# A hybrid attention layer: PSUM banks, activation tables and the place of four kinds of work on the engines

## The chip, the cores and the metric

One core of a Trainium2 chip runs the kernel; the other seven do nothing. The metric is the device time of one launch in microseconds, the median of three runs. Engines, as the profile names them: PE (TensorE, matrix products, with PEld for its weight loads), DVE (VectorE), ACT (ScalarE), POOL (GpSimd) and SP (SyncE, which here issues every DMA).

## The reference

x has 4096 rows of 1024 columns. It is modulated, `h = x * (1 + scale) + shift`, with shift, scale and a gate from `c @ w_ada + b_ada`, and projected by `h @ w_in` (3608 columns). Two kinds of attention run over chunks, each with 4 heads on half the width:

- Gated attention: `g = log_sigmoid(z) / 16` decays a state per key column. With b the running sum of g in a chunk of 64, the output is `tril((q e^(b-bref)) (k e^(bref-b))^T) v + (q e^b) S`, and `S = e^(b_last) S + (k e^(b_last-b))^T v`.
- Delta rule: q, k, v pass a causal convolution of width 4 and Silu, q and k are normalised; one decay per head and step. With `L = exp(d_i - d_j)` under the diagonal, `A = (beta k k^T) * L` strictly under it, each chunk solves `(A + I) [u, w] = [v beta, k beta e^d]`, then `v_new = u - w S`, `o = (q e^d) S + (q k^T * L) v_new`, `S = e^(d_last) S + (k e^(d_last-d))^T v_new`.

Each head's output is divided by its root mean square and multiplied by a weight and `silu` of a gate projection. Both halves together go through `w_out`, and the result is `layer_norm(alpha x + (1 + gate) y)`. All in float32.

## The kernel before, in words

The sequence is cut into 8 blocks of 512 rows (`NB`, `TB`). Products of the projections are made in three passes over a high and a low part of each operand (`mm3`), eight slices of 128 columns per sum (`KT`); one step of a query, key or convolution projection is three matrix products of 512 columns. PSUM has 8 banks; `share_banks` (L57) splits them into projection banks and work banks.

Phase 1, gated attention: 16 blocks, first all 8 with t = 0 (heads 0 and 1), then all 8 with t = 1. For t = 0, `make_h` (L213) loads x in four tiles, `mod_split` (L201) modulates each slice and splits it into two parts, and `keep_h` writes h to DRAM for the 24 later reads (`load_h`, L225). `block` (L586) makes values, then the gate's low-rank rows `lr` (transposed for t = 0 and stored; loaded and cast for t = 1), `decays` (the exponentials), queries, keys and gates, and ends in two Silus of `sg`. `chunks` (L488) and `finish` (L511) do the recurrence of the block before: eight chunk steps, each a product whose result one copy on DVE writes into the next step's operand and one copy on ACT into o; then sums of squares on ACT, a power on POOL, four transposes per half and the product with the gate. `first_block` (L537) makes block 0's eight sums while the modulation's weights and x arrive; its eight banks are three projection and five work banks.

Phase 2, the delta rule: again 16 blocks, each over several iterations. In iteration `it`, block `it` is new, block `it-1` is solved and scanned, block `it-2` is normalised. `first_half` (L989) is woven with the key and query projections (`qk_products`, 32 steps), `second_half` (L1010) with values and gates (`vg_products`). The tile E holds L of the new block: a load, a mask on POOL, eight exponentials on ACT (`decay_tiles`, L743); `gram` (L790) multiplies it into the products AQ, whose diagonal blocks are inverted on DVE after a round trip through DRAM (U, R, Rd). `inverse_head` and `inverse` (L835, L848) put the inverse together from small products, with copies of Pa and Rt on ACT between them; `scan` (L898) runs the recurrence.

Phase 3: products with `w_out`, and the layer norm per 128 rows (`out_block`, L682).

What sets the order: `weave` (L243) takes a generator of side work and one of projections; a side yield of n lets n projection steps pass before the side's next products. On PE the side's products are kept behind the projection products written before them while the projections last. ACT's functions of different tables are kept in written order (`in_order`, L82); a table that the written code does not load is loaded just ahead of its use. All else, every queue's order included, is chosen when the kernel is built by a scheduler that takes the written order, free buffers and its own durations; on the chip each engine then runs its queue in that order, and SP issues DMAs in its order. A tile whose tag has one buffer waits until the last reader of the tile before it is done: `lr_raw` shares the tag `la` with e1 (L394, L417), E and U share `EU`.

Of the kernel before, what the change touches and what calls it, by code (L numbers as in the profile page):

```python
# [13 lines left out]
F32 = mybir.dt.float32  # L14
# [16 lines left out]
def tile_hybrid(ctx, tc, xp, x, c, wada, bada, w_gla, w_vl, w_gdn, w_out, wup, bgate,  # L31
# [78 lines left out]

    def copy_a(out, in_):
        nc.scalar.copy(out=out, in_=in_)  # L112
# [88 lines left out]
    def mod_split(xt, k):  # L201
        j = k % 2
        nc.vector.tensor_scalar(out=xt[:, j], in0=xt[:, j], scalar1=modc[:, 8 + k:9 + k],
                                scalar2=modc[:, k:k + 1], op0=mul, op1=add)
        t = pair(hpool)
        return split(xt[:, j], (t[:, 0], t[:, 1])), t
# [6 lines left out]
    def make_h(b):  # L213
        h, tiles = [], []
        for kk in range(4):
            xt = xpool.tile([P, 2, TB], F32, name="xt", tag="x")
            nc.sync.dma_start(out=xt, in_=xp[b, kk])
            for j in range(2):
                parts, t = mod_split(xt, 2 * kk + j)
                h.append(parts)  # L220
                tiles.append(t)
        keep_h(b, tiles)
        return h
# [111 lines left out]
    with ExitStack() as ph:  # L335
        share_banks(ph, 3)
# [48 lines left out]
        def lr_rows(t, b):  # L385
            lr = gp.tile([80, TB], F32R, name="lr", tag="lr")
            if t == 0:
                pt = work_psum()
                for g in range(4):
                    transpose(pt[0:80, g * P:(g + 1) * P], in_=lrt[:, g].bitcast(F32), identity=ident)  # L390
                copy_a(lr, pt[0:80])
                nc.sync.dma_start(out=lrsp[b], in_=lr.bitcast(F32))
            else:
                raw = gp.tile([P, TB], F32, name="lr_raw", tag="la")[0:80]  # L394
                nc.sync.dma_start(out=raw, in_=lrsp[b])
                copy_a(lr, raw)
            return lr
# [74 lines left out]
        def values(t, b, wv, h, VS):  # L472

            nw = 256 if t else 280
            for gg in range(2):
                vps = [proj_psum() for _ in range(2)]
                for k in range(KT):
                    for j in range(2):
                        values_k(vps[j][:, 0:nw], wv, h, k, 2 * gg + j)
                    yield  # L480
                for j in range(2):
                    v_out(t, b, VS, 2 * gg + j, vps[j])
# [5 lines left out]
        def chunks(W, VS, VS_next, o, ss):  # L488

            o8 = o.rearrange("p g (h v) -> p (g h) v", h=2)  # L490
            for n in range(8):
                g, r = n // 2, n % 2
                pm = work_psum()
                for hh in range(2):
                    mm(pm[:, hh * P:(hh + 1) * P], lhsT=W[:, g, r, hh, :],
                                     rhs=VS[:, g, r, hh * P:(hh + 1) * P], start=True, stop=True)
                if r == 0:
                    nc.vector.tensor_copy(out=VS[0:64, g, 1, :], in_=pm[0:64, 0:256])  # L498
                    copy_a(o[64:128, g, :], pm[64:128, 0:256])
                else:  # L500
                    if g < 3:
                        nc.vector.tensor_copy(out=VS[64:128, g + 1, 0, :], in_=pm[64:128, 0:256])  # L502
                    elif VS_next is not None:
                        nc.vector.tensor_copy(out=VS_next[64:128, 0, 0, :], in_=pm[64:128, 0:256])
                    copy_a(o[0:64, g, :], pm[0:64, 0:256])
                    for j in (2 * g, 2 * g + 1):
                        jk = gp.tile([P, P], F32, name="jk", tag="jk")
                        act(jk, o8[:, j], AF.Square, accum_out=ss[:, j:j + 1])
                yield 2
# [25 lines left out]
        small = []  # L535

        def first_block():  # L537

            h, tiles, wt = [], [], {}
            ps = [proj_psum() for _ in range(3)] + [work_psum() for _ in range(8 - 3)]  # L540
            xt = None
            for k in range(KT):
# [18 lines left out]
                tiles.append(t)  # L561
            keep_h(0, tiles)
# [23 lines left out]
        def block(t, b, h, W, VS, sg, first):  # L586
# [11 lines left out]
            e1, e2, e3, e4 = decays(t, lr_rows(t, b))  # L598
# [10 lines left out]
            kt_, kh = scale_k(pk, e2, e4)  # L609
            pg = [proj_psum() for _ in range(2)] if first is None else first[6:8]  # L610
# [12 lines left out]
        def before(st, VS):  # L623
# [4 lines left out]
            yield from chunks(st["W"], st["VS"], VS, o, ss)  # L628
# [7 lines left out]
        for it in range(2 * NB + 1):  # L636
# [10 lines left out]
            if new:  # L647
# [5 lines left out]
                h = make_h(it + 1) if it + 1 < NB else load_h((it + 1) % NB)  # L653
# [28 lines left out]
    def out_block(b, y, xres, lnw_sb, lnb_sb):  # L682
        for g in range(4):
# [23 lines left out]
            nc.vector.tensor_scalar(out=xt, in0=xt, scalar1=mv[:, 0:1], scalar2=rl, op0=sub, op1=mul)  # L707
            tt(xt, xt, lnw_sb, mul)
            tt(xt, xt, lnb_sb, add)
            nc.sync.dma_start(out=out[r0:r0 + P], in_=xt)  # L710


    with ExitStack() as ph:
# [29 lines left out]
        def decay_tiles(t, b, E):  # L743
# [3 lines left out]
            load_table()  # L747
            for cc in range(2):
# [4 lines left out]
                for n in range(4 * cc, 4 * cc + 4):  # L753
                    act(E[:, n], E[:, n], AF.Exp, bias=dneg[:, t, c0 + n:c0 + n + 1])
# [93 lines left out]
        def inverse(st):  # L848
# [15 lines left out]
            yield 2  # L864
# [124 lines left out]
        def first_half(new, last, done):  # L989
# [15 lines left out]
            if last is not None:  # L1005

                yield 4 if done is not None else 10
                yield from inverse(last)

# [145 lines left out]
```

## Time and profile before

| what | value |
|---|---|
| median of three runs | 2152.29 us (2149.45 to 2164.0) |
| the profiled execution | 2148.5 us, span of the trace 2146.8 us |
| PE busy | 2064.2 us, 96% of the span |
| DVE busy | 1320.7 us, 62% |
| ACT busy | 956.6 us, 45% |
| POOL busy | 228.1 us, 11% |
| mean granted clock of PE | 0.988 of full speed |

The span runs from the first to the last instruction. A busy time is the union of an engine's instructions; matrix products overlap in the pipeline, so idle time of PE in this table is time in which it had nothing to run. In the page's 40 slices, gated attention fills about the first 13 (to some 700 us), the delta rule the next 22 (to some 1860 us), and the output the rest.

### The profile page before, as it was taken

The numbers are of one execution on the slowest core, as the hardware profiler recorded it, in microseconds if no ns is written. First come the engines' busy times: TensorE is split into PE (matmuls) and PEld (weight loads), VectorE is DVE, ScalarE is ACT, GpSimd is POOL, SyncE is SP. The second block draws the span as 40 slices with busy tenths as digits, with TensorE's granted clock in tenths as the row PEclk, the third lists the DMA queues.
The fourth block names the chain that finished last, engine by engine and source line by source line (L and its number), as shares of the span: only waits on it lengthen the run. The fifth ranks groups of instructions, "written<-read, shape, count | busy, mean of one in ns | idle before, by whom it ended". The sixth has DMA issues, their size and how long they took to land.

```text
span 2146.8 us, 34571 instructions
## 1 busy us (share of the span) xinstructions
PE 2064.2 (96%) x12809; PEld 1743.0 (81%) x12809; DVE 1320.7 (62%) x3181; ACT 956.6 (45%) x2563; POOL 228.1 (11%) x430
## 2 busy tenths in 40 slices
PE   6899999999999999999999999999999999999998
PEld 5788888888888778887888878888888888788886
DVE  7785666445335676655666666665566666676665
ACT  2655555544454544554535665445544463121110
POOL 1000000000000221111210212101221110000000
PEclk9999999999999999998999999999999999999999
DMA  8575336423423544331332443333123354353321
GB/s 316 193 254 203 141 134 227 157 102 107 168 92 118 203 172 163 95 96 46 114 116 92 139 151 104 116 103 95 56 94 116 124 182 140 140 210 143 136 103 76
DMA packets 118585, 297.17 MB, mean 138 GB/s; under 512 B 45920, under 2 KB 48144, under 8 KB 117392
## 3 DMA queue, kind: packets, MB, share of 16 engines
q1 hardware_dynamic: 118416, 294.95, 40.1%
q8 instruction: 101, 1.65, 0.3%
q14 instruction: 68, 0.56, 0.1%
HBM read 213.84 MB, written 81.07 MB: 137 GB/s over the span
## 4 chain that ended last, share of the span: by engine, by line
PE 64%; DVE 11%; ACT 9%; DMA 8%; issue 3%; POOL 2%; SPq 2%; POOLq 0%; DVEq 0%; ACTq 0%
PE pp L98 48%; PE pw L98 15%; DMA lr_raw<-lr_spill 2%; ACT jk L104 2%; PE pw L101 2%; DMA xt<-xp 2%; ACT E L104 2%; DMA r_spill<-R 1%; DVE tp L69 1%; DVE R L69 1%; ACT L104 1%; DVE vp L69 1%; DMA Rd<-r_spill 1%; DVE cacc L72 1%; DVE W L69 1%
## 5 line engine op out<-in xcount | busy, mean ns | idle before, releaser
L98 PE MATMUL pp<-h,w 128*128 128x512 f32 x4512 | 1158.9, 402 | 1.2 <-DVE W L69 1.2
L98 PEld LDWEIGHTS pp<-h,w 128*128 128x128 f32 x4512 | 824.1, 189 | 157.8 <-issue 2.0
L98 PE MATMUL pp<-w,h 128*128 128x512 f32 (+1 forms) x2112 | 421.5, 355 | 11.8 <-ACT sg L104 10.6
L98 PEld LDWEIGHTS pp<-w,h 128*128 128x128 f32 x2112 | 349.1, 189 | 65.7 <-ACT sg L104 12.0
L72 DVE SCALAR_TENSOR_TENSOR cacc<-u,convw_sb,cacc 128x512 f32<-128x512 f32 x288 | 217.4, 756 | 127.0 <-ACT cacc L104 122.2
L98 PE MATMUL pp<-wvl,h 128*128 128x280 f32 x744 | 119.9, 310 | 34.9 <-ACT h L112 26.3
L98 PEld LDWEIGHTS pp<-wvl,h 128*128 128x128 f32 x744 | 105.6, 198 | 38.7 <-ACT h L112 29.4
L69 DVE TENSOR_TENSOR tp<-U,R 128x60 f32<-128x60 f32 (+24 forms) x496 | 104.3, 210 | 14.7 <-DMA U<-u_spill 3.0
L69 DVE TENSOR_TENSOR R<-R,tp 128x60 f32<-128x60 f32 (+24 forms) x496 | 104.2, 210 | 12.8
L498 DVE COPY VS<-pw 64x256 f32<-64x256 f32 x64 | 26.7, 417 | 135.5 <-PE pw L98 135.1
L112 ACT COPY u<-pp 128x512 f32<-128x512 f32 x96 | 55.9, 582 | 119.8 <-PE pp L98 109.9
L104 ACT ACTIVATE rl<-mv,lnepscol 128x1 f32<-128x1 f32 x32 | 9.4, 294 | 217.9 <-DVE mv L703 215.8
L261 POOL TENSOR_TENSOR rs<-ss,minus_half 128x8 f32<-128x8 f32 x16 | 31.4, 1962 | 606.7 <-DVE ss L514 606.7
L98 PE MATMUL pw<-S,KQ 128*128 128x128 f32 x512 | 84.4, 278 | 0.0
L98 PE MATMUL pw<-VS,W 128*128 128x128 f32 x512 | 81.3, 282 | 1.2 <-DVE VS L498 0.9
L104 ACT ACTIVATE jk<-pw 128x128 f32<-128x128 f32 x256 | 70.5, 276 | 26.5 <-PE pw L101 20.3
L72 DVE SCALAR_TENSOR_TENSOR S<-S,edl,pw 128x128 f32<-128x128 f32 x128 | 42.4, 344 | 61.6 <-PE pw L98 61.5
L98 PEld LDWEIGHTS pw<-S,KQ 128*128 128x128 f32 x512 | 74.0, 191 | 6.3 <-DVE S L72 2.4
L104 ACT ACTIVATE jk<-vp 128x128 f32<-128x128 f32 x128 | 39.9, 311 | 84.7 <-DVE vp L69 82.7
L72 DVE SCALAR_TENSOR_TENSOR xres<-xres,pp 128x512 f32<-128x512 f32 x48 | 32.4, 684 | 70.9 <-PE pp L98 66.7
L112 ACT COPY o<-pw 64x256 f32<-64x256 f32 x128 | 46.8, 366 | 63.7 <-DVE VS L502 33.8
L98 PEld LDWEIGHTS pw<-VS,W 128*128 128x128 f32 x512 | 70.6, 196 | 4.2 <-DVE VS L502 0.9
(287 smaller groups left out, 2759.0 us busy)
## 6 DMA issues: line engine op xcount, KB each, us to landing
h<-h_spill SPq DMA_DIRECT2D x192, 512.0 KB
h_spill<-h SPq DMA_DIRECT2D x64, 512.0 KB
xt<-xp SPq DMA_DIRECT2D x32, 512.0 KB
y_spill<-sg SPq DMA_DIRECT2D x32, 512.0 KB
yt<-y_spill SPq DMA_DIRECT2D x32, 512.0 KB
xres<-x SPq DMA_DIRECT2D x24, 512.0 KB
out_dram<-xres SPq DMA_DIRECT2D x24, 512.0 KB
mt<-wada SPq DMA_DIRECT2D x8, 1024.0 KB
```

The costliest lines, as they stand in the source:

```text
L69: nc.vector.tensor_tensor(out=out, in0=a, in1=b, op=op)
L72: nc.vector.scalar_tensor_tensor(out=out, in0=a, scalar=s, in1=b, op0=op0, op1=op1)
L98: pe(nc.tensor.matmul(out, lhsT=lhsT, rhs=rhs, start=start, stop=stop))
L101: pe(nc.tensor.transpose(out, in_=in_, identity=identity))
L104: ins = nc.scalar.activation(out=out, in_=in_, func=func, **kw)
L112: nc.scalar.copy(out=out, in_=in_)
L261: nc.gpsimd.tensor_tensor(out=y, in0=x, in1=e, op=ALU.pow)
L498: nc.vector.tensor_copy(out=VS[0:64, g, 1, :], in_=pm[0:64, 0:256])
```

## The change

Gated attention: four projection banks and four work banks instead of three and five, and the first block's value sums take the four work banks; the Silu table is loaded right behind the exponentials; the modulation of x moves from DVE to ACT; `lr` is loaded without a cast for t = 1, and its store for t = 0 comes behind `scale_k`; values are made as one pair of groups and two single ones; squares move from ACT to POOL with a sum on DVE; a chunk step lets 3 projection steps pass for t = 0 (before 2). Two x loads of block 1 are issued ahead of the stores of block 0's h. Delta rule: the eight exponentials of E and their table load move from the place of the mask to the end of the first half; one yield of the inverse is 3 instead of 2. Output: the normalisation is two operations instead of three, and in halves for the last 128 rows.

```diff
@@ -107,6 +107,9 @@
         in_order(nc.scalar.preload_act_table_set("natural_log_exp_and_others"))
+    def load_silu():
+        in_order(nc.scalar.preload_act_table_set("silu_and_others"))
@@ -200,8 +203,7 @@
         j = k % 2
-        nc.vector.tensor_scalar(out=xt[:, j], in0=xt[:, j], scalar1=modc[:, 8 + k:9 + k],
-                                scalar2=modc[:, k:k + 1], op0=mul, op1=add)
+        act(xt[:, j], xt[:, j], AF.Identity, scale=modc[:, 8 + k:9 + k], bias=modc[:, k:k + 1])
@@ -210,11 +212,15 @@
-    def make_h(b):
+    def load_x(b, kk):
+        xt = xpool.tile([P, 2, TB], F32, name="xt", tag="x")
+        nc.sync.dma_start(out=xt, in_=xp[b, kk])
+        return xt
+    def make_h(b, ahead=()):
         for kk in range(4):
-            xt = xpool.tile([P, 2, TB], F32, name="xt", tag="x")
-            nc.sync.dma_start(out=xt, in_=xp[b, kk])
+            xt = ahead[kk] if kk < len(ahead) else load_x(b, kk)
@@ -333,7 +339,7 @@
     with ExitStack() as ph:
-        share_banks(ph, 3)
+        share_banks(ph, 4)
@@ -389,11 +395,8 @@
                 copy_a(lr, pt[0:80])
-                nc.sync.dma_start(out=lrsp[b], in_=lr.bitcast(F32))
             else:
-                raw = gp.tile([P, TB], F32, name="lr_raw", tag="la")[0:80]
-                nc.sync.dma_start(out=raw, in_=lrsp[b])
-                copy_a(lr, raw)
+                nc.sync.dma_start(out=lr.bitcast(F32), in_=lrsp[b])
@@ -472,22 +475,27 @@
             nw = 256 if t else 280
-            for gg in range(2):
-                vps = [proj_psum() for _ in range(2)]
+            vps = [proj_psum() for _ in range(2)]
+            for k in range(KT):
+                for j in range(2):
+                    values_k(vps[j][:, 0:nw], wv, h, k, j)
+                yield
+            for j in range(2):
+                v_out(t, b, VS, j, vps[j])
+            for g in range(2, 4):
+                ps = proj_psum()
                 for k in range(KT):
-                    for j in range(2):
-                        values_k(vps[j][:, 0:nw], wv, h, k, 2 * gg + j)
-                    yield
-                for j in range(2):
-                    v_out(t, b, VS, 2 * gg + j, vps[j])
+                    values_k(ps[:, 0:nw], wv, h, k, g)
+                    if k % 2:
+                        yield
+                v_out(t, b, VS, g, ps)
-        def chunks(W, VS, VS_next, o, ss):
-            o8 = o.rearrange("p g (h v) -> p (g h) v", h=2)
+        def chunks(W, VS, VS_next, o, ss, steps):
@@ -503,10 +511,11 @@
                     copy_a(o[0:64, g, :], pm[0:64, 0:256])
-                    for j in (2 * g, 2 * g + 1):
-                        jk = gp.tile([P, P], F32, name="jk", tag="jk")
-                        act(jk, o8[:, j], AF.Square, accum_out=ss[:, j:j + 1])
-                yield 2
+                    sq = gp2.tile([P, 2, P], F32, name="sq", tag="sq")
+                    o2 = o[:, g].rearrange("p (h v) -> p h v", h=2)
+                    nc.gpsimd.tensor_tensor(out=sq, in0=o2, in1=o2, op=mul)
+                    nc.vector.tensor_reduce(out=ss[:, 2 * g:2 * g + 2], in_=sq, op=add, axis=mybir.AxisListType.X)
+                yield steps
@@ -532,12 +541,12 @@
-        small = []
+        small, x_next = [], []
             h, tiles, wt = [], [], {}
-            ps = [proj_psum() for _ in range(3)] + [work_psum() for _ in range(8 - 3)]
+            ps = [work_psum() for _ in range(4)] + [proj_psum() for _ in range(4)]
@@ -559,6 +568,7 @@
                 tiles.append(t)
+            x_next.extend(load_x(1, kk) for kk in range(2))
@@ -595,7 +605,9 @@
                     v_out(t, b, VS, g, first[g])
-            e1, e2, e3, e4 = decays(t, lr_rows(t, b))
+            lr = lr_rows(t, b)
+            e1, e2, e3, e4 = decays(t, lr)
+            load_silu()
@@ -607,6 +619,8 @@
             kt_, kh = scale_k(pk, e2, e4)
+            if t == 0:
+                nc.sync.dma_start(out=lrsp[b], in_=lr.bitcast(F32))
@@ -625,7 +639,7 @@
             yield 2
-            yield from chunks(st["W"], st["VS"], VS, o, ss)
+            yield from chunks(st["W"], st["VS"], VS, o, ss, 2 if st["t"] else 3)
@@ -650,7 +664,7 @@
                     gate_scalars()
-                h = make_h(it + 1) if it + 1 < NB else load_h((it + 1) % NB)
+                h = make_h(it + 1, x_next if it == 0 else ()) if it + 1 < NB else load_h((it + 1) % NB)
@@ -704,10 +718,11 @@
             act(rl, rl, AF.Exp, scale=-0.5)
-            nc.vector.tensor_scalar(out=xt, in0=xt, scalar1=mv[:, 0:1], scalar2=rl, op0=sub, op1=mul)
-            tt(xt, xt, lnw_sb, mul)
-            tt(xt, xt, lnb_sb, add)
-            nc.sync.dma_start(out=out[r0:r0 + P], in_=xt)
+            for cs in [slice(0, D)] if r0 + P < T else [slice(0, TB), slice(TB, D)]:
+                stt(xt[:, cs], xt[:, cs], mv[:, 0:1], lnw_sb[:, cs], sub, mul)
+                stt(xt[:, cs], xt[:, cs], rl, lnb_sb[:, cs], mul, add)
+                nc.sync.dma_start(out=out[r0:r0 + P, cs], in_=xt[:, cs])
@@ -744,14 +759,17 @@
             nc.sync.dma_start(out=E.rearrange("p n c -> p (n c)"), in_=dsp[t, b:b + 1].to_broadcast([P, 8 * P]))
-            load_table()
                                         pattern=[[0, 4], [1, P]], channel_multiplier=-1)
-                for n in range(4 * cc, 4 * cc + 4):
-                    act(E[:, n], E[:, n], AF.Exp, bias=dneg[:, t, c0 + n:c0 + n + 1])
+        def decay_exps(t, b, E):
+            c0 = 8 * b
+            load_table()
+            for n in range(8):
+                act(E[:, n], E[:, n], AF.Exp, bias=dneg[:, t, c0 + n:c0 + n + 1])
@@ -861,7 +879,7 @@
                 copy_a(Pa[q[2 * i + 1]], pp[i][q[2 * i + 1]])
-            yield 2
+            yield 3
@@ -1006,6 +1024,8 @@
                 yield from inverse(last)
+            if new is not None:
+                decay_exps(new["t"], new["b"], new["E"])
```

## Rows read from the trace of the kernel before

**Rows 1.** Stretches: length; busy PE, PEld, DVE, ACT, POOL (count); clock; DMA share, GB/s.

```profile
61.50:84.00 22.50, 15.35 (x111) 14.05 (x112) 20.16 (x39) 14.55 (x25) 0.00 (x0) 0.77 0.65 227
...
150.00:370.00 220.00, 213.00 (x1430) 186.35 (x1429) 146.21 (x324) 124.49 (x279) 8.99 (x8) 0.99 0.47 174
370.00:700.00 330.00, 317.48 (x2117) 280.28 (x2116) 142.20 (x280) 154.64 (x383) 18.05 (x8) 0.99 0.36 128
...
872.00:1860.00 988.00, 974.38 (x6344) 811.74 (x6342) 628.74 (x1813) 483.95 (x1425) 151.57 (x321) 0.99 0.36 114
...
sum 2146.80, PE 2064.21 PEld 1743.01 DVE 1320.68 ACT 956.62 POOL 228.09; mean PE 229.36 PEld 193.67 DVE 146.74 ACT 106.29 POOL 25.34
```

**Rows 2.** PE's waits: us in total, times, longest us.

```profile
PE pw L98 <- ACT Pa L112: 11.5, 15, 1.6
PE pp L98 <- ACT sg L104: 10.6, 7, 2.5
PE pp L98 <- ACT o L112: 6.4, 4, 2.1
```

**Rows 3.** Timeline, a block's end, t = 1: start, duration, instruction, count [idle before <-releaser].

```profile
501.60 0.62 ACT L112 CAST lr<-lr_raw 80x512 fp32r<-80x512 f32 x1 [5.59 <-DMA lr_raw<-lr_spill]
502.24 1.28 ACT L104 ACT_TABLE_LOAD   x1
503.54 1.09 ACT L104 ACTIVATE sg<-pp 128x512 f32<-128x512 f32 x2
...
504.18 0.98 PE L98 MATMUL pp<-w,h 128*128 128x256 f32 x6 [1.12 <-ACT sg L104]
```

**Rows 4.** Timeline, 202 to 217 us, ACT in the values, t = 0.

```profile
212.67 0.62 ACT L112 CAST h<-xt 128x512 fp32r<-128x512 f32 x1 [0.99 <-DMA xt<-xp]
```

**Rows 5.** Groups by form: shapes, busy us, mean ns, idle before.

```profile
L104 ACT ACTIVATE la<-la,onecol 128x512 f32<-128x512 f32 x16 | 11.5, 720 | 0.3
```

**Rows 6.** Timeline, 0 to 70 us, DVE beside POOL.

```profile
11.47 1.67 DVE L203 TENSOR_SCALAR xt<-xt,modc 128x512 f32<-128x512 f32 x1
11.49 1.36 POOL L360 TENSOR_TENSOR wvl<-raw,wvl 128x560 fp32r<-128x560 f32 x1 [8.48 <-ACT wvl L112]
```

**Rows 7.** Timeline, 2128 to 2147 us and 2143 to 2147 us, the end.

```profile
2137.58 0.69 DVE L72 SCALAR_TENSOR_TENSOR xres<-xres,pp 128x512 f32<-128x512 f32 x1 [3.96 <-PE pp L98]
...
2139.84 0.81 DVE L707 TENSOR_SCALAR xres<-xres,mv,rl 128x1024 f32<-128x1024 f32 x1 [0.60 <-ACT rl L104]
...
2143.19 0.33 SPq L710 DMA_DIRECT2D out_dram<-xres  x1
```

**Rows 8.** Timeline, 505 to 512 us, chunk steps (t = 1).

```profile
506.87 0.43 DVE L502 COPY VS<-pw 64x256 f32<-64x256 f32 x1 [0.80 <-PE pw L98]
...
508.10 0.61 PE L98 MATMUL pw<-VS,W 128*128 128x128 f32 x4
```

**Rows 9.** Timeline, 54 to 90 us, from_q of block 0.

```profile
69.57 1.73 DVE L69 TENSOR_TENSOR W<-pw,e 64x256 f32<-64x256 f32 x4
```

**Rows 10.** Timeline, 1108 to 1142 us, ACT ahead of Pa.

```profile
1126.68 1.28 ACT L109 ACT_TABLE_LOAD   x1
...
1127.97 2.46 ACT L104 ACTIVATE E<-E,dneg 128x128 f32<-128x128 f32 x8
...
1134.15 1.28 ACT L104 ACT_TABLE_LOAD   x1
...
1136.77 0.60 PE L98 MATMUL pw<-Rd,Pa 32*32 32x32 f32 x9 [1.17 <-ACT Pa L112]
```

**Rows 11.** Timeline, 1142 to 1175 us, last KQ and first AQ.

```profile
1142.78 0.62 ACT L104 ACTIVATE KQ<-cacc 128x512 f32<-128x512 f32 x1
...
1144.25 1.66 DVE L72 SCALAR_TENSOR_TENSOR AQ<-pw,f__11191,E 128x256 f32<-128x256 f32 x4 [3.50 <-PE pw L98]
```

**Rows 12.** Busy time of ACT, granted clock, 1143.4 to 1154.4 us.

```profile
1143.40:1154.40 11.00, 4.53 (x20) 1.00 0.21 48
```

**Rows 13.** Busy time of each engine and granted clock, 998 to 1014 us.

```profile
998.00:1014.00 16.00, 14.86 (x103) 11.61 (x104) 5.89 (x13) 5.41 (x13) 1.96 (x3) 0.57 0.00 1
```

## The prediction

> **What bounds the kernel now.** I read the stages first: TensorE is busy 2064.21 us of a 2146.80 us span [rows 1], so all its waiting together is 82.6 us, and no edit on another engine can give more than its share of that. By stage: 7.2 us of waiting in 61.5 to 84 (end of the first block), 7.0 in 150 to 370 (gated attention, t = 0), 12.5 in 370 to 700 (t = 1), 13.6 in 872 to 1860 (delta rule). The rest is the start, which waits for the first loads, the end behind the last product, and places that the change does not aim at. Then TensorE's waits by who ended them [rows 2]: leaving aside the h tiles, most of which are the first ones, three ScalarE tiles lead, Pa (11.5 us in 15 waits), sg (10.6 us in 7) and o (6.4 us in 4). The change touches what stands ahead of each on ScalarE's queue.
>
> **The change part by part.**
>
> *Gated attention, t = 1 (sg).* At a block's end ScalarE casts the loaded rows lr (waiting 5.59 us for their load), loads the Silu table (1.28) and runs the two Silus (1.09); TensorE has one free bank, fills it with 12 products and then stands 1.12 us until the first Silu frees one [rows 3]. The change takes away all three causes: the load goes straight into lr (the cast is gone, and the load has its own tile, no longer the one that e1 holds until the block's end), the Silu table is loaded behind the exponentials, and a fourth bank lets the next values start. I take the whole sg wait, 10.6 us. What is late next: nothing on ScalarE before the next o copy. The fourth bank is taken from the work banks (5 to 4); the largest need at once is three in from_k, or two at the gate transposes.
>
> *t = 0 (o).* A cast of the next h, held 0.99 us by its x load, stands ahead of the VS and o copies on ScalarE, and those free banks [rows 4]. With four projection banks no values group waits for an earlier group's copy, and at three steps a chunk instead of two the state copy has one more step of six products; 6.4 us of o waits would go, I take 6. Moving the modulation puts 64 operations more on ScalarE. Nearest rows: the cast of 80x512 at 0.62 [rows 3] and a 128x512 operation with one column operand at 0.72 [rows 5]; a second column operand may add the same 0.10 again, so 0.62 to 0.82, I take 0.72, the nearer in kind: 5.8 us a block. The squares that leave are not counted against it. ScalarE is busy 124.49 of 220 us there [rows 1], so this is hidden; if that cover were gone it would cost 8 blocks x 5.8 = 46. The loads of x now stop ScalarE instead of VectorE, and behind them stand the copies just named; the fourth bank is what covers that.
>
> *Squares on GpSimd.* By elements, 256/560 of the 1.36 us row gives 0.62 us for each of 64, then a VectorE sum near 0.4. GpSimd is nearly idle. The price is on VectorE: its modulation of 128x512 took 1.67 us beside the GpSimd operation that began 0.02 later [rows 6], where another operation of that size takes 0.69 [rows 7], so a VectorE operation can be held for all of it. Where it hit a state copy of a chunk: the copy of 0.43 us starts at 506.87 and the chunk that reads it at 508.10 [rows 8], a slack of 0.80, more than 0.62. I take 0, bound 3 us.
>
> *First block.* Two x loads of block 1 are issued ahead of eight h_spill issues, but its value banks are now work banks and the query, key and gate sums hold all four projection banks. Block 1 can start only when from_q has read the queries (its last read ended at 71.30 [rows 9]) or a Silu has read a gate; VectorE no longer modulates, so about 70. Before, block 1 had banks early and stood for h. So the two edits work against each other: of 7.2 us I take 2, between -3 and +7. The lr_spill store moves behind scale_k on SyncE's queue; its reader comes eight blocks later, so 0. The spill of the gated output issues later for t = 0, since chunks and finish take 8 more steps; x loads queued behind it wait for tiles freed at the same time, 0, bound 4 us over 7 blocks.
>
> *Delta rule, exponentials last.* In the first half ScalarE runs, without a gap, table load 1.28, eight exponentials 2.46, then copies and squares, table load 1.28, Silu, and only then the Pa copies; TensorE stands 1.17 us for them at 1136.77 [rows 10]. That is 5.02 us ahead of Pa that leave. The waits for Pa are 1.6 at most each, so all 11.5 us go; I take 11. Where they come back: the chain is now fourth KQ Silu's end 1143.40, load to 1144.68, first pair of exponentials 1145.30, last 1147.14. The products AQ that read E start at 1144.25 after VectorE had been idle 3.50 us [rows 11]; they would be 1.05 late, and no more at the end, since a product takes 0.42 and an exponential 0.31. ScalarE is idle 11.00 - 4.53 = 6.5 us between that Silu and the z copy at 1154.40 [rows 12], more than 5.02. So 0, with a bound of 5.02 in each of 15 blocks. The step of the inverse raised from 2 to 3 does nothing: by then the side has taken 31 steps (10+1+1, 1+1, 3, 8, 2, 4) of 32, and both 2 and 3 run the main part out.
>
> *Clock.* In 998 to 1014 the granted clock is 0.57 [rows 13], part of it at the lower level of 1.2 GHz, after a Pa wait of 1.6 us; at 0.57 a stretch of 16 us loses up to 6.9. Other waits of that size show no fall, so I count 3 of it, between 0 and 7.
>
> *Tail.* From 2139.84 to the issue at 2143.19 three operations; now two of 0.69 for each half [rows 7]: 4 x 0.69 = 2.8 against 3.35, with the first no longer waiting for rl and the last store half as large, so 1 us. The other row blocks' shorter normalisation is hidden by products.
>
> *Sum:* 10.6 + 6 + 2 + 11 + 3 + 1 = 33.6, 34 us, on a profiled execution of 2148.5 us (span 2146.8): 2114.5. The median shown is 2152.29, 3.8 above that execution, so I predict 2118.
>
> **The rivals.** *The waits move (no change).* The order on each engine is chosen anew at build time, so other operations may meet; the fall of o and sg may give way to ScalarE standing for x with Silu and copies behind it. The cast of [rows 4] speaks for it, the idle time of ScalarE and the fourth bank against. If the t = 0 gain and the first block's are lost (8), VectorE's collisions cost 3 and a fifth of the 46 us shows (9), 34 - 8 - 3 - 9 = 14 us are left: about 2138. *The exponentials become the bound (slower).* Place: AQ waits for E, the gram sums keep four of five work banks, and the scan's products queue behind them. Price: 5.02 us in 15 blocks, 75 us, and the 11 + 3 us of gain gone: 2152.3 - 20 + 75 = 2207. It decides from 2.8 us a block ((21.5 + 20)/15); the idle 3.50 us ahead of AQ speaks against. *A table load holds ScalarE longer than its row (less gain).* Place: the two loads that now stand between the fourth Silu and the first vT. Over the 5.02 us there are 1.5 left; each us beyond comes back in 15 blocks, 15 us. In the row at 502.24 the Silu follows its load's end by 0.02 [rows 3], so this has a small chance, and at 1.3 us over the time would be 2118 + 20 = 2138. The Trainium skill (ScalarE: Activation LUTs, What ACT_TABLE_LOAD costs) gives each switch a drain of about 1.38 us besides its 1.28, so two of them would take 2.8 us more, 1.3 over what is left; the row does not show such a drain. *More than forecast:* all of the first block's 7, the whole 6.9 of clock, and the early loads too: 34 + 5 + 4 + some of the slow clock near 62 to 84 (granted 0.77, up to 5): about 2105 or below. *It does not do what it says:* for the inverse step and the early x loads that is my forecast already.
>
> **How the numbers follow.** About 1% (21.5 us) is what this measurement tells from no change: faster is below 2130.8, slower above 2173.8. Forecast (26 to 42 us gained, 2110 to 2126) 0.45; more than forecast 0.17; waits move, 2126 to 2152, 0.27, of which a sixth is still below 2130.8; longer loads 0.03; exponentials or another new bound 0.08. So faster 0.67, same 0.26, slower 0.07. Range: 2096 to 2146, which leaves out the slower case and the far ends of two others.
>
> **What would show it.** In t = 1, no sg wait on TensorE and no lr cast on ScalarE; in the delta rule, Pa copies right behind their products and no Pa wait, exponentials between the fourth Silu and the first vT, and AQ's first pair about 1 us later against its sums. TensorE idle in 872 to 1860 near 3 us, in 370 to 700 near 2. It would be wrong if TensorE waited for AQ, z or E in the second half, if ScalarE's modulation stood for x with VS or o copies behind it and TensorE behind those, or if block 1 started later than 73 us.

## The result and the profile after

The changed kernel took 2123.05 us (2120.95 to 2125.33, three runs) against 2152.29 before: ratio 0.9845, interval 0.9816 to 0.9875. The forecast was 2118 in 2096 to 2146. The profiled executions differ less, 2146.8 to 2123.6 us of span: the one shown after was the slowest of its three, and the one before (2148.5 us) was faster than all three runs before.

For the parts I use landmarks on TensorE: the first 64x64 product of each from_k (16, one per block of gated attention), the first gram sum of each block of the delta rule (16), and the last product.

| stretch | before, us | after, us | gain | forecast |
|---|---|---|---|---|
| start to first from_k | 73.8 | 71.3 | 2.5 | 2 |
| from_k 1 to 8 (t = 0) | 294.3 | 302.0 | -7.7 | 6 |
| from_k 8 to 16 (t = 1) | 333.7 | 321.5 | 12.2 | 10.6 |
| from_k 16 to gram sum 1 | 42.9 | 43.3 | -0.4 | 0 |
| gram sum 1 to 16 | 992.8 | 977.1 | 15.7 | 14 |
| gram sum 16 to last product | 400.0 | 400.9 | -0.9 | 0 |
| behind the last product | 9.2 | 7.4 | 1.8 | 1 |

One part failed, t = 0, and it failed with the wrong sign. The stretches of the changed kernel, with the columns of [rows 1]:

```profile
61.50:84.00 22.50, 14.87 (x128) 14.37 (x129) 17.17 (x36) 18.74 (x32) 0.75 (x2) 0.77 0.85 293
150.00:370.00 220.00, 209.65 (x1384) 183.59 (x1383) 133.59 (x298) 130.52 (x231) 23.77 (x29) 0.99 0.47 170
370.00:700.00 330.00, 325.47 (x2228) 287.54 (x2227) 167.08 (x329) 129.13 (x249) 35.31 (x41) 0.99 0.39 139
872.00:1860.00 988.00, 978.87 (x6394) 815.08 (x6395) 636.63 (x1817) 486.01 (x1427) 156.41 (x319) 1.00 0.36 115
998.00:1014.00 16.00, 16.00 (x87) 13.79 (x86) 8.33 (x20) 11.68 (x38) 0.56 (x3) 1.00 0.18 43
```

TensorE's waiting in 150 to 370 rose from 7.0 to 10.4 us; in 370 to 700 it fell from 12.5 to 4.5, in 872 to 1860 from 13.6 to 9.1; the prediction's signs for the last two were 2 and 3. The clock of 0.57 in 998 to 1014 [rows 13] is now 1.00. Of TensorE's waits in [rows 2], sg and o are gone over the whole run, and Pa nearly (0.5 us, once). In their place stand lrt, e and VS, VectorE's tiles, most of it in t = 0. All that TensorE waited for in 100 to 373 us:

```profile
PE pw L101 <- DVE lrt L69: 6.5, 10, 0.9
PE pw L98 <- DVE VS L510: 2.4, 3, 1.3
PE pw L98 <- ACT h L115: 2.2, 3, 0.8
PE pw L98 <- DVE e L69: 1.9, 2, 1.3
PE pw L101 <- DVE e L69: 1.1, 1, 1.1
PE pw L98 <- DVE VS L506: 1.0, 2, 0.7
```

**What t = 0 waits for.** The values of one block in the timeline of the changed kernel, ScalarE, GpSimd, VectorE and TensorE in turn (start, duration, instruction, count, idle before and releaser):

```profile
216.37 2.94 ACT L104 ACTIVATE xt<-xt,modc 128x512 f32<-128x512 f32 x4 [1.91 <-DMA xt<-xp]
219.33 0.37 ACT L115 COPY o<-pw 64x256 f32<-64x256 f32 x1
219.59 0.75 ACT L115 COPY VS<-pp 64x256 f32<-64x256 f32 x2
...
219.83 0.62 POOL L516 TENSOR_TENSOR sq<-o 128x256 f32<-128x256 f32 x1 [6.78 <-ACT o L115]
...
220.48 0.42 DVE L517 TENSOR_REDUCE ss<-sq 128x2 f32<-128x256 f32 x1 [4.10 <-POOL sq L516]
220.94 0.19 DVE L387 CAST lrt<-pp 128x32 fp32r<-128x32 f32 x1
...
221.39 0.31 PE L101 MATMUL pw<-ident,lrt 128*80 128x128 f32 x1 [0.94 <-DVE lrt L69]
...
222.92 0.19 DVE L387 CAST lrt<-pp 128x32 fp32r<-128x32 f32 x1 [1.19 <-ACT VS L115]
```

Read it downwards: ScalarE stands 1.91 us for a load of x, then modulates four times; the o copy and two VS copies wait behind that; the square on GpSimd waits for the o copy; the sum on VectorE waits for the square, and VectorE, which goes in order, is idle 4.10 us in front of it; an lr copy stands behind the sum, and TensorE waits for it. The Trainium skill says the same of the queues (PSUM — Partial Sum Buffer, Engine vs sequencer instructions: ScalarE's, VectorE's and GpSimd's are strictly first in, first out), and this trace agrees. But the sum holds this lr copy only a little: in no kernel of this record does an lr copy start less than 0.03 us behind the second VS copy of its group, which ends here at 220.34, against 220.90 for the sum; and the next lr copy (222.92) waits for its VS copies by name. So what holds the lr copies is mostly the VS copies, which stand behind ScalarE's modulations; what the sum costs shows at another place, below.

**t = 1.** The end of a block, which answers to [rows 3]:

```profile
504.12 1.28 ACT L104 ACTIVATE sg<-pp 128x512 f32<-128x512 f32 x2 [4.97 <-PE pp L98]
...
504.60 1.59 PE L98 MATMUL pp<-w,h 128*128 128x256 f32 x12
```

No cast and no load of a table stands ahead of the Silus; ScalarE waits 4.97 us for TensorE and not the other way round.

**Delta rule.** The stretch that answers to [rows 10, 11], with the first TensorE product behind the 32x32 ones; then, of the kernel before, that product, and the first 32x32 product that needs the second Pa copy:

```profile
1121.00 0.76 ACT L115 COPY Pa<-pw 32x256 f32<-32x256 f32 x2 [1.28 <-PE pw L98]
...
1125.59 0.63 ACT L104 ACTIVATE KQ<-cacc 128x512 f32<-128x512 f32 x1 [0.25 <-DVE cacc L72]
1126.95 0.59 ACT L104 ACTIVATE Rt<-pw 64x512 f32<-64x512 f32 x1 [0.74 <-PE pw L98]
1127.56 1.28 ACT L109 ACT_TABLE_LOAD   x1
1128.86 2.45 ACT L104 ACTIVATE E<-E,dneg 128x128 f32<-128x128 f32 x8
...
1129.93 0.88 DVE L72 SCALAR_TENSOR_TENSOR AQ<-pw,f__11118,E 128x256 f32<-128x256 f32 x2 [4.37 <-ACT E L104]
...
1121.79 0.23 PE L98 MATMUL pw<-Rd,Pa 32*32 32x32 f32 x2
...
1122.43 0.97 PE L98 MATMUL pp<-h,w 128*128 128x512 f32 x3
```

```profile
1137.17 0.21 PE L98 MATMUL pw<-Pa,Rd 32*32 32x32 f32 x1
...
1137.79 1.20 PE L98 MATMUL pp<-h,w 128*128 128x512 f32 x4
```

```profile
L112 ACT COPY Pa<-pw x2: 363/364/364, 1136.4 to 1136.7; 32x256 f32<-32x256 f32 x2
```

ScalarE now waits 1.28 us for the products that Pa copies, and TensorE waits for no Pa. The 48 small products that read Pa take 0.64 us (1121.79 to 1122.43) where they took 1.02 (1136.77 [rows 10] to 1137.79): before, nine of them ran behind the first Pa copy and the others waited for the second, which ended at 1137.1 (tile Pa in the kernel before: duration smallest, median and largest in ns, first and last start). The first sum of this block began at 1128.80, so AQ follows its first sum by 1.13 us; before it was 2.07 (1142.18 to 1144.25). AQ became earlier, not later.

**Tail.** Against [rows 7]: the two halves' normalisation, on VectorE:

```profile
2117.93 1.42 DVE L72 SCALAR_TENSOR_TENSOR xres<-xres,mv,lnw_ln 128x512 f32<-128x512 f32 x2
2119.26 1.41 DVE L72 SCALAR_TENSOR_TENSOR xres<-xres,rl,lnb_ln 128x512 f32<-128x512 f32 x2
```

The four operations take 2.83 us (2.8 forecast), and the first no longer waits for rl; the stretch behind the last product is 1.8 us shorter.

### The profile page after: what moved, and what is told of

The parts are those of the page before. It is cut to its first block, busy times and chain, and to the rows that moved or that the text cites. A ratio compares the mean times of both kernels' runs of the same rounds, so it can differ in the third digit from the quotient of the medians.

```text
span 2123.6 us, 34530 instructions
## 1 busy us (share of the span) xinstructions
PE 2053.0 (97%) x12809; PEld 1733.9 (82%) x12809; DVE 1306.3 (62%) x3151; ACT 952.1 (45%) x2363; POOL 273.1 (13%) x494
## 4 chain that ended last, share of the span: by engine, by line
PE 73%; DVE 11%; DMA 6%; ACT 4%; issue 3%; POOL 2%; SPq 1%; DVEq 0%; POOLq 0%; ACTq 0%
PE pp L98 56%; PE pw L98 14%; PE pw L101 3%; DVE W L69 1%; DVE R L69 1%; DVE tp L69 1%; DMA mt<-wada 1%; DMA xt<-xp 1%; DVE e L69 1%; DMA wt<-wada 1%; DVE cacc L72 1%; DVE vp L69 1%; DMA r_spill<-R 1%; POOL rs L267 1%; DMA Rd<-r_spill 1%
## 5 line engine op out<-in xcount | busy, mean ns | idle before, releaser
L98 PE MATMUL pp<-h,w 128*128 128x512 f32 x4608 | 1189.3, 403 | 0.4 <-DVE w L69 0.4
L98 PEld LDWEIGHTS pp<-h,w 128*128 128x128 f32 x4608 | 840.1, 189 | 158.0 <-DVE w L69 0.8
L516 POOL TENSOR_TENSOR sq<-o 128x256 f32<-128x256 f32 x64 | 44.8, 700 | 574.7 <-ACT o L115 569.2
L98 PE MATMUL pp<-wvl,h 128*128 128x280 f32 x672 | 97.9, 298 | 8.2 <-DVE W L69 8.2
L98 PEld LDWEIGHTS pp<-wvl,h 128*128 128x128 f32 x672 | 89.9, 191 | 8.9 <-issue 8.5
L98 PEld LDWEIGHTS pw<-S,KQ 128*128 128x128 f32 x512 | 73.8, 191 | 6.3 <-DVE S L72 2.6
L104 ACT ACTIVATE KQ<-cacc 128x512 f32<-128x512 f32 x64 | 40.3, 630 | 83.7 <-DVE cacc L72 83.3
L104 ACT ACTIVATE sg<-pp 128x512 f32<-128x512 f32 x64 | 37.5, 598 | 87.8 <-PE pp L98 85.7
```

The costliest lines, as they stand in the source:

```text
L98: pe(nc.tensor.matmul(out, lhsT=lhsT, rhs=rhs, start=start, stop=stop))
L104: ins = nc.scalar.activation(out=out, in_=in_, func=func, **kw)
L516: nc.gpsimd.tensor_tensor(out=sq, in0=o2, in1=o2, op=mul)
```

## The experiments

Times are medians; each ratio is against the kernel before on the same chip. "t = 0" and "t = 1" are the landmarks' stretches in the profiled execution.

**Four for t = 0.** The edits, in this order: the modulation back on VectorE, the squares back on ScalarE, two steps a chunk, and all three.

```
 e1_mod_vec
-        act(xt[:, j], xt[:, j], AF.Identity, scale=..., bias=...)
+        nc.vector.tensor_scalar(out=xt[:, j], in0=xt[:, j], ..., op0=mul, op1=add)
 e2_sq_act
-                    nc.gpsimd.tensor_tensor(out=sq, in0=o2, in1=o2, op=mul)
-                    nc.vector.tensor_reduce(out=ss[:, 2 * g:2 * g + 2], in_=sq, ...)
+                    for j in (2 * g, 2 * g + 1):
+                        act(jk, o8[:, j], AF.Square, accum_out=ss[:, j:j + 1])
 e3_step2
-            yield from chunks(..., 2 if st["t"] else 3)
+            yield from chunks(..., 2)
 e4_t0_back: the three together
```

> The changed kernel with the modulation of x back on VectorE, all else as changed. From the first from_k to the eighth (t = 0) the changed kernel took 302.0 us, the kernel before 294.3. Theory A (ScalarE stops at the modulation for a load of x, and the o copies, by way of the squares and their sums, hold the lr copies behind it): t = 0 comes down to 294 us or below, TensorE's 6.5 us of waiting for the lr tile goes, the time falls by 8 us or more, to about 2115. Theory B (the squares' way over GpSimd and back to VectorE is what holds the lr copies, whoever modulates): t = 0 falls by 2 us at most. Theory C (three steps a chunk put the chunk's copies against the values' copies): nothing changes within 2 us.

> The changed kernel with the squares of o back on ScalarE with its own accumulation. Theory A (modulation standing for x): the lr copies no longer wait for a sum behind GpSimd, but ScalarE is still stopped by x, with the o and VS copies behind it, and it has about 4 us a block more to do: t = 0 stays at 300 to 305 us. Theory B (the way over GpSimd): t = 0 falls to 296 or below, TensorE's waits for the lr tile (6.5 us) go, the time falls by 6 to 8 us. Theory C: nothing within 2 us. In t = 1 (321.5 us) all theories expect at most 1 us more.

> The changed kernel with two steps of the main part a chunk in t = 0, as before, in place of three. Theory C (three steps put the chunks' copies of state and output against the values' copies, which free the banks): t = 0 falls from 302 to about 294 us. Theories A and B: the same loads and the same way over GpSimd meet the same copies a little earlier; t = 0 changes by less than 3 us, with either sign.

> The changed kernel with all three undone: modulation on VectorE, squares on ScalarE, two steps a chunk; the four projection banks and the values in single banks stay. If these three are the whole of what t = 0 lost, t = 0 is at 294 us or below, and if the fourth bank takes the 6.4 us of o waits as forecast, at 288: the time 2109 to 2115. If t = 0 stays above 298, its loss lies in the fourth bank or in the values in single banks, which put 12 products of one bank behind each other.

A fifth was run later, the squares on ScalarE and two steps, with the modulation left on ScalarE:

```
 e11_sq_step = e2_sq_act + e3_step2
```

> The changed kernel with the squares back on ScalarE and two steps a chunk, the modulation on ScalarE. Squares alone undone gave t = 0 = 292.3 us, all three undone 292.2. If the place of the modulation costs 2.9 us by itself, as when it alone was undone, t = 0 is at 295; if it matters only together with the squares' way over GpSimd, at 292 or below. Time 2104 to 2117, by how often TensorE's clock falls at the start of the delta rule.

| kernel | modulation | squares | steps | t = 0 | t = 0, clock at full | time | ratio |
|---|---|---|---|---|---|---|---|
| before (3 banks) | VectorE | ScalarE | 2 | 294.3 | 290.3 | 2152 | 1 |
| changed | ScalarE | GpSimd | 3 | 302.0 | 299.2 | 2123.05 | 0.9845 (0.9816 to 0.9875) |
| e1 | VectorE | GpSimd | 3 | 299.2 | 297.3 | 2125.53 | 0.9884 (0.9838 to 0.9930) |
| e3 | ScalarE | GpSimd | 2 | 303.7 | 296.6 | 2124.44 | 0.9878 (0.9838 to 0.9917) |
| e2 | ScalarE | ScalarE | 3 | 292.3 | 290.2 | 2116.38 | 0.9839 (0.9797 to 0.9881) |
| e11 | ScalarE | ScalarE | 2 | 298.9 | 297.5 | 2112.69 | 0.9814 (0.9779 to 0.9850) |
| e4 | VectorE | ScalarE | 2 | 292.2 | 290.7 | 2104.51 | 0.9788 (0.9749 to 0.9826) |

The sixth column is an estimate: it takes off the half of the time in which the records have the clock at the lower level (8.0 us of the stretch before, 5.6 after, 2.8 to 14.2 in the others). It tells stretches apart to about 1.5 us, since e5 below, whose gated attention is that of the kernel before, has 291.8 against 290.3. In size theory B stands: undoing the squares alone takes 9.0 us off t = 0 (299.2 to 290.2). Theory A in its plain form falls, and so does C: with the squares on GpSimd the modulation's place is worth 1.9 us and the steps 2.6. But the three are not independent. With two steps the squares' place is worth nothing (e3 296.6, e11 297.5; both values expected for e11 were lower). With the squares on ScalarE, modulation on ScalarE wants three steps (290.2 against 297.5), and modulation on VectorE does as well with two (290.7). These are single profiled executions; by time x mean clock over four runs each, e11 lies only some 4 us above e2. The times stand in another order, since in e2's profiled execution the clock was at the lower level for 31 us at the start of the delta rule and in e4's and e11's not at all there; time x mean clock is 2093 to 2099 in e2, 2098 to 2102 in e11, 2089 to 2099 in e4.

All waits for 100 to 373 us in e2, then the first two for 100 to 370 us in e11:

```profile
PE pw L101 <- DVE lrt L69: 6.2, 7, 1.6
PE pw L98 <- DVE VS L511: 1.6, 3, 0.9
PE pw L98 <- DVE VS L507: 0.8, 2, 0.6
PE pw L101 <- DVE e L69: 0.6, 1, 0.6
```

```profile
PE pw L101 <- DVE lrt L69: 6.7, 6, 1.3
PE pw L98 <- ACT VS L115: 4.5, 3, 1.8
```

So theory B's way was wrong: it said that the lr waits go with the squares, and they stay (6.5 to 6.2). What goes are the waits at from_k (h and e in the list of the changed kernel), from 5.2 us in six to 0.6 in one, and 1.0 us of VS waits. One from_k, VectorE and TensorE, in the changed kernel and in e2:

```profile
188.28 1.73 DVE L69 TENSOR_TENSOR W<-pp,e 64x256 f32<-64x256 f32 x4
...
191.66 0.42 DVE L517 TENSOR_REDUCE ss<-sq 128x2 f32<-128x256 f32 x1
...
194.49 1.23 DVE L69 TENSOR_TENSOR o<-o,rs 128x1024 f32<-128x1024 f32 x1 [1.75 <-POOL rs L267]
195.75 1.29 DVE L69 TENSOR_TENSOR e<-pp,e 128x512 f32<-128x512 f32 x2
...
196.59 0.69 PE L98 MATMUL pw<-e,e 64*64 64x64 f32 x32 [0.77 <-ACT h L115]
```

```profile
187.25 1.73 DVE L69 TENSOR_TENSOR W<-pp,e 64x256 f32<-64x256 f32 x4
...
192.72 1.23 DVE L69 TENSOR_TENSOR o<-o,rs 128x1024 f32<-128x1024 f32 x1 [1.81 <-POOL rs L267]
193.98 1.29 DVE L69 TENSOR_TENSOR e<-pp,e 128x512 f32<-128x512 f32 x2
...
194.92 0.69 PE L98 MATMUL pw<-e,e 64*64 64x64 f32 x32
```

In all six waits the product starts 0.15 us behind the end of an e operation (in five of them the first of the two), also where the profile names h. At three steps the last sum and the normalisation of o, which waits for GpSimd's power, stand in VectorE's queue ahead of e. From the first W operation to the end of e VectorE takes 8.76 us in five blocks of the changed kernel against 8.0 in e2: the sum adds 0.45, and one W operation beside the square took 0.74 instead of 0.42. That 0.75 us is about the wait. At two steps the normalisation comes behind e and the way takes 6.33 in most blocks, with either place of the squares (e3, e11). These waits make up some 6 of the 9.0 us; the rest is not assigned.

What three steps give back is the VS wait in e11's list. There ScalarE stands 2.71 us for x at 212.24 with an o copy and the VS copies behind it, and the chunk's product at 215.05 waits 1.78 us for VS: the condition that the prediction named as a way to be wrong. Nor did the fourth bank give its 6 us. In e4, which differs from the kernel before in t = 0 by the banks, the single-bank groups, the early table, the early x loads and the later lr store, the o waits are gone, yet t = 0 is no shorter (290.7 and 290.3 at full clock); the chunks wait for the state copies instead:

```profile
PE pw L98 <- DVE VS L512: 5.5, 4, 1.6
```

The lr waits are 1.5 us there.

**The delta rule alone.** The kernel before with only the exponentials moved:

```
-            load_table()
             for cc in range(2): ... affine_select ...
-                for n in range(4 * cc, 4 * cc + 4):
-                    act(E[:, n], E[:, n], AF.Exp, bias=...)
 ...
                 yield from inverse(last)
+            if new is not None:
+                decay_exps(new["t"], new["b"], new["E"])
```

> The kernel before with only the decay exponentials moved to the end of the half; gated attention, tail and inverse step as before. From the third gram sum to the sixteenth (13 blocks of the delta rule) the kernel before took 865.1 us, the changed one 843.4. Theory A (the Pa waits, with what is lost inside the 32x32 products that follow them, and the fall of clock behind one of them): this edit alone gives the whole of it, 844 to 848, with TensorE's Pa waits (11.5 us) below 1 us and no wait for AQ or z above 1 us a block; the time falls by 17 to 21 us, to about 2133. Theory B (my forecast as written): 11 us of waits and 3 of clock, 851. Theory C (part of the stretch's gain is from banks, tables or the queue left by the other edits): 855 or more.

2134.33 us, ratio 0.9900 (0.9848 to 0.9951). Gram sum 3 to 16 took 839.4 us against 865.1. Of the 25.7 us, 6.8 are the clock (13.7 us at the lower level in the kernel before, none here); 18.9 are the edit. The stretch is even below the 844 to 848 of theory A. The first two blocks pay a part of it back: from gram sum 1 to 16, at full clock, 984.3 us became 969.2 here and 970.3 in the changed kernel, 14 to 15. All that TensorE waited for in 872 to 1740 us:

```profile
PE pw L98 <- ACT TP L104: 1.9, 10, 0.2
PE pw L98 <- DVE Td L842: 1.7, 2, 1.3
PE pw L101 <- DVE vp L69: 1.5, 2, 1.2
PE pw L101 <- ACT KQ L104: 0.3, 1, 0.3
```

The Pa waits (some 11 us) are gone, but the waits for TP and Td (3.6) are new, so the waiting fell by some 7.8. The 48 products behind the Pa copies took 1.01 us in most blocks against 0.64 here: 0.37 x 13 = 4.8 more, an estimate. Some 6 us of the 18.9 stay unassigned.

**Which of three causes held sg.** The Silu table loaded late again; three projection banks again; and both, so that only the cast is gone.

```
 e6_silu_late
-            load_silu()
 e7_banks3
-        share_banks(ph, 4)
+        share_banks(ph, 3)
-            ps = [work_psum() for _ in range(4)] + [proj_psum() for _ in range(4)]
+            ps = [proj_psum() for _ in range(3)] + [work_psum() for _ in range(8 - 3)]
 e12_cast_only = e7_banks3 + e6_silu_late
```

> The changed kernel without the early load of the Silu table, so that it is loaded ahead of the block's two Silus as before (1.28 us each). t = 1 took 333.7 us before and 321.5 after. Theory A (the load on the way to the Silus holds the bank): part of the sg wait returns, 0.5 to 1.2 us a block, t = 1 at 325 to 331. Theory B (four banks and the missing cast suffice; the early load is not needed): t = 1 within 1.5 us of 321.5. In t = 0 both expect less than 2 us of change.

> The changed kernel with three projection banks and five work banks as before, the first block's sums placed as before. Theory A (the fourth bank is what frees TensorE at a block's end in t = 1): the sg wait returns in part, t = 1 at 325 to 332 in place of 321.5. Theory B (the cast and the table load were the cause): t = 1 within 1.5 us. First block: the next block's values have banks early again, so TensorE's wait of 8.2 us before 69 us shrinks by 2 to 5 us if the banks were the cause, and not at all if the next h tiles were. t = 0: the VS copies free a bank each, so 2 to 8 us longer than 302.0.

> The changed kernel with three projection banks and the Silu table loaded late, both as before: of the three things meant to free sg in t = 1 only the direct load of lr is left. Theory A (the cast of lr, which stood for its load of 5.59 us ahead of the Silus, was the whole cause): t = 1 stays at 320 to 322 with no sg wait. Theory B (any two of the three suffice, but one does not): t = 1 at 325 to 331, sg waits of 0.4 to 1 us a block.

e6: 2120.68 us, 0.9841 (0.9794 to 0.9889), t = 1 321.3. e7: 2124.20, 0.9865 (0.9806 to 0.9924), t = 1 319.9. e12: 2123.27, 0.9860 (0.9817 to 0.9902), t = 1 321.6. The changed kernel had 321.5 and the kernel before 333.7, and in none of the three does TensorE wait for sg. So of the three, taking away the cast, which stood for its load ahead of the Silus, is enough; the early table and the fourth bank were not needed. The values' new grouping and the squares on GpSimd are in all three kernels, and no run puts the cast back alone. ScalarE stood idle for 5.59 us ahead of the cast [rows 3], so less work on ScalarE ahead of it can't have freed sg; the grouping is not ruled out.

In t = 0 the fourth bank does seem to count beside the rest of the change: from the second from_k to the eighth, at full clock, e7 and e12 with three banks took 270.6 and 268.7 us, the changed kernel and e6 with four 265.8 and 264.7. Over the whole of t = 0 the earlier start of block 1 in e7 and e12 (next experiment) hides it.

**First block.** Its eight sums shared out so that two projection banks come free with the values:

```
-            ps = [work_psum() for _ in range(4)] + [proj_psum() for _ in range(4)]
+            ps = [(proj_psum, work_psum)[int(c)]() for c in "00111001"]
```

> The changed kernel with the first block's eight sums shared out otherwise over the four projection and four work banks: two value groups, the keys and one gate in projection banks, two value groups, the queries and one gate in work banks. So two projection banks are free as soon as the values are copied. Theory A (as in the prediction: the next block waits for banks, not for its h): TensorE's wait of 8.2 us that ends at 68.96 falls to 3 us or less, and the second from_k comes 4 to 7 us earlier than 105.8. Theory B (the next h is what is late, since ScalarE modulates most of it only from 70 us on): the second from_k comes 0 to 2 us earlier. Later stages unchanged in both.

2118.42 us, 0.9845 (0.9793 to 0.9897). From the first from_k to the second 32.4 us, with e7's old placing 31.9, against 34.5. TensorE in the gap, in the changed kernel, in e8 and in e7:

```profile
68.96 2.21 PE L98 MATMUL pp<-wvl,h 128*128 128x280 f32 x8 [8.19 <-DVE W L69]
```

```profile
60.62 2.48 PE L98 MATMUL pp<-wvl,h 128*128 128x280 f32 x18
69.89 1.30 PE L98 MATMUL pp<-wvl,h 128*128 128x280 f32 x4 [6.79 <-ACT sg L104]
```

```profile
61.14 4.03 PE L98 MATMUL pp<-wvl,h 128*128 128x280 f32 x30
71.87 1.13 PE L98 MATMUL pw<-e,e 64*64 64x64 f32 x32 [6.70 <-DVE e L69]
```

Block 1 did wait for banks: where they are free it starts before 60.62 and 61.14. But theory A's size was wrong. TensorE runs 18 or 30 more products and then waits 6.8 us for a gate's bank or 6.7 for e, so 2 to 3 us come of it, not 4 to 7.

**A version meant to beat both.** All that helped, together; and the same with the lr transposes two steps later in t = 0:

```
 e9_best = e4_t0_back + e8_first, and in the first block alone
+            act(xt[:, j], xt[:, j], AF.Identity, scale=..., bias=...)
 e10_best_lr = e9_best, and
+            k0 = 2 if first is None and t == 0 else 0
+            for k in range(k0):
+                proj_k(pq, wq, h, k)
+                yield
             lr = lr_rows(t, b)
```

> A version meant to beat both: the changed kernel with the squares on ScalarE, two steps a chunk, the modulation on ScalarE in the first block alone and on VectorE after it, and the first block's sums shared out over both kinds of banks so that two projection banks come free early. If the parts add: the kernel with the three undone took 2104.5 us, its first from_k came at 73.3 us (71.4 with the first modulation on ScalarE), and the other placing of the sums gave 2.1 us up to the second from_k: about 2100 us, t = 0 at 289 to 292. If the gains don't add, 2104 to 2108.

> The version before it in this set, and in t = 0 the transposes of lr two steps of the query sums later, so that six products each lie between the last lr copy and the transposes. Theory (TensorE's waits for the lr tile are lost only because nothing stands between): those waits (1.5 us in the kernel with three undone, 6.2 with the squares alone undone) go, t = 0 falls by 1 to 4 us. Rival (the decays' chain behind lr starts 2.4 us later, and from_q or from_k then waits for e): t = 0 stays or grows by up to 10 us.

e9: 2103.95 us, 0.9774 (0.9744 to 0.9803). e10: 2102.00, 0.9765 (0.9735 to 0.9795), t = 0 290.3. Both beat the changed kernel, whose interval starts at 0.9816; against e4 and each other their gain is within the intervals. At full clock t = 0 is 288.8 in both against 290.7 in e4, and in e9 that gain lies between the first two from_k (31.2 against 33.1), where e8 had it. So the first block's 2 us seem to add, though that is near what such stretches tell apart, and the later transposes give nothing that can be told.

## Why the prediction was near, and the step that failed

That the total came within 5 us of the forecast is partly luck. The forecast was 31 us for the edits and 3 for the clock; by time x mean clock (last section) the edits gave some 19 and the clock some 10, so a clock better than I counted stood in for some 7 of the us that the edits fell short.

*sg: right in size (10.6 forecast, 12.2 measured), too wide in cause.* I counted three causes, of which one was enough.

*t = 0: the failed step.* The prediction said of the squares: "I take 0, bound 3 us", and of the o waits: "I take 6", and it added the parts as if each stood alone. For the squares I had priced only a VectorE operation that runs beside GpSimd, at a state copy with 0.80 us of slack. The cost is elsewhere: at three steps a chunk the sum stands in VectorE's queue ahead of the scaled keys e, and from_k waits for those. At three steps, with modulation on ScalarE, moving the squares cost 9.0 us of t = 0, some 6 of it in waits that can be named; at two steps it cost nothing. GpSimd's own time was as forecast (0.62 us in the row above, estimate 0.62). The modulation was not hidden as I had it: ScalarE standing for x holds the VS copies and, with them, the lr copies (with only the modulation undone, in e1, the lr waits fall from 6.5 to 3.0 us) and, at two steps, the chunks (e11). For the o waits I took a wait's disappearance for its gain: in e4 they vanish and nothing is won, since the state copies are late next. The rival "the waits move" had this kind of loss: 6 + 9 + 3 us for t = 0, where forecast and measurement came to differ by 13.7.

*First block: right* in cause (banks, from_q, about 70; it ended at 68.96) and size (2 forecast, 2.5 up to the first from_k), though TensorE's waiting in 61.5 to 84 did not fall (7.2 to 7.6 us). Some 2 us of the 2.5 come with the modulation on ScalarE: in e1 and e4, with it on VectorE, the first from_k comes at 73.4 and 73.3, not 71.3. No run undoes the early x loads.

*Delta rule: right in direction, the Pa term too small* (11 taken; 14 to 15 over all blocks at full clock, 18.9 from the third sum on). The list of waits gave the idle time before the first product only; the products behind it stood once more, for the second Pa copy. And AQ was not 1.05 us late: I had left the fourth Silu at its old place, but it comes forward once 5.02 us ahead of it are gone. The rival of exponentials as the bound failed for that: the last of them ends at 1131.31, and the sums' last pair is read at 1134.60. The rival of a longer table load failed too: the exponentials start 0.02 us behind the load's end (1127.56 + 1.28), and the load 0.02 behind the Rt copy's. The Trainium skill's drain of about 1.38 us (ScalarE: Activation LUTs, What ACT_TABLE_LOAD costs) shows on neither side, so here the measurement decides against it.

*The inverse's step from 2 to 3: nothing, as forecast.* The kernel e5 keeps 2, and from the third gram sum to the fifteenth TensorE, VectorE, ScalarE and GpSimd run the same instructions in the same order as in the changed kernel.

*Clock: the fall at 1000 us went, but another grew in its place* at 862, behind a wait of 1.5 us for Td (3.4 us at the lower level near there before, 13.7 after):

```profile
861.93:875.59 13.66, 13.66 (x100) 10.28 (x99) 3.13 (x5) 6.41 (x12) 0.37 (x2) 0.50 0.00 1
```

So the profiled pair gained little from it, and the runs some: the mean granted clock of the after runs was 0.991 to 0.993, of 25 runs of before beside the experiments 0.980 to 0.994, 0.987 in the middle.

## What to carry to other kernels

Before moving work to an idle engine, write down the new instruction that has to fetch the result back, and look for what stands behind it in its engine's queue: that pays, however short the work itself is. A stage's waits that disappear are a gain only if the producer that is late next is named and later than needed; undo parts one by one, in pairs too, since an edit (the squares or the chunk steps here) can be worth nothing or 7 to 9 us depending on another. A part that helps when undone need not work the way its theory says: look whether the wait that the theory names is the one that went. Price a removed wait by the stretch from the last product before it to the first one behind its dependents.

## What the runs showed of the hardware beside that

The clock is a large part of the spread between runs: before's runs went from 2140.14 us at a mean clock of 0.994 to 2168.82 at 0.980, and time x clock of those two is 2127 and 2125. Over the 25 runs of before it is 2119 to 2131, 2126 in the middle. The changed kernel has 2106 to 2108, some 19 us less, so some 10 of the 29 go with the clock. A wait of about 1.5 us does not settle whether it falls: behind the wait for Td of 1.5 us it did, behind one of 1.8 us at the same place in e10 it did not.
